# Weight loads pinned to program order in a one-core decoder layer: raw blocks, wide blocks and kept pairs on SyncE's queue

## The chip, the cores and the metric

The kernel runs on one core of a Trainium2 chip. The metric is the device time of one execution in microseconds (us), as the median of several runs. Beside it stands one profiled execution, from which all durations are read.

## The reference

One step of a one-layer hybrid decoder: a prompt of 2048 tokens and 8 samples of 4 tokens, model width 1024, all in float32. Cut to what matters here:

```python
def decoder_layer(x, p, lp, state):
    xn = rms_norm(x, lp['norm_mix_pre'])
    qk_raw, v_m, o_m, gates, q_a, k_a, v_a = split_projection(xn @ lp['w_in'])
    ...                                    # short_conv, heads
    (c_new, n_new, m_new), h = mlstm_prompt(q, k, v, ig, lf)      # or mlstm_chunk on the state
    att = swa_prompt(q_a, k_a, v_a, lp['attn_sinks'])             # or swa_sample on the cache
    y_m = mlstm_output(h, o_m, lp['mlstm_norm'])
    y_a = rms_norm(att.astype(x.dtype), lp['attn_norm'])
    mix = jnp.concatenate([y_m, y_a], axis=-1) @ lp['w_out']
    x = x + rms_norm(mix, lp['norm_mix_post'])
    u = rms_norm(x, lp['norm_ffn_pre'])
    f = jnp.square(jax.nn.relu(u @ lp['w_up'])) @ lp['w_down']
    x = x + rms_norm(f, lp['norm_ffn_post'])
    x = x + jax.nn.sigmoid(x @ lp['w_pgate']) * (p @ lp['w_pproj'])
```

The outputs are the rows of both inputs after the layer, and the new states of both.

## The kernel before, in words

**Stages.** The 16 blocks of 128 prompt rows form six chunks (four of three blocks, two of two). The first part of the kernel runs over the six chunks: norm, the product with w_in, the attention heads and the recurrent heads, whose results go to DRAM (up to about 660 us of the profile). The second part runs over three groups of two chunks. A group goes through the product with w_out (`mix_mm`, matmuls `mo`), the norm behind it (DVE lines 1468 and 1485), the MLP (`mlp`: 16 steps of 256 hidden columns, matmuls `up` and `dn`) and the gate (`gate_mm`, matmuls `pg` and `pv`). The 32 sample rows run beside the prompt: their attention beside group 1, the rest beside the last group.

**Weights.** TensorE reads each weight as a pair of fp32r tiles (high part and rest). `Ring` makes and feeds them. The first time a weight is used, a raw block is loaded from its input (lines 351 to 385; 5 raw buffers), ACT rounds it (line 254) and DVE or POOL subtracts (line 255). If it is used again, POOL stores the pair to DRAM (line 282, `wk<-w`), and every later use is a single load of this kept pair of 512 KB (line 289, `w<-wk`) into one of 7 pair tiles. From the third step of a group's MLP on, the `up` weights of group 0 come from wide blocks of w_up (line 307, four buffers), of which seven sums per step are made on DVE and POOL.

**Queues and order.** All these loads are issued by SyncE (SP in the profile), as are the rows of x (line 477), the decay matrices of the recurrent heads (`Wt<-mbd`, line 961), the gains of the norms behind mix and MLP (`gpost`, `gffn`, line 1453), the rows of p (line 1875) and the last chunk's results (line 1833: `ot` of a prompt block, `ots` of the sample rows). SP takes its instructions in order; one that waits for a buffer or for data holds up all behind it. The kernel's text gives a first order. A scheduler ahead of the run moves instructions of one engine past one another where it expects that to be earlier; `here = tc.keep_in_program_order` takes one instruction out of that and leaves it behind the one that stood just before it on its engine in the text. TensorE's instructions, the subtractions and the stores of pairs are all pinned so; DMAs of SP are not.

**Single buffers beside the ring.** The pool `gp` has one buffer for a gain: the load of `gffn` waits until the last DVE instruction that reads `gpost` (line 1468) has ended. In the text `mlp` asks for `gffn` in its first line, ahead of its first weight:

```python
    gp = es2.enter_context(tc.tile_pool(name="gp", bufs=1, reuse_waits="tile"))
    def mlp(gi, chunks, sample):
        gffn = gain(A["norm_ffn_post"], f"gffn{gi}")
```

In the gate of a chunk, the text has the weights of half 0 (8 of w_pgate, 2 of w_pproj), the results of half 0 (`finish`, whose store waits for ACT and DVE), and then the weights and results of half 1.

Of the kernel before, what the change touches and what calls it, by code (L numbers as in the profile page):

```python
# [11 lines left out]
U32 = mybir.dt.uint32  # L12
# [6 lines left out]
P = 128  # L19
# [11 lines left out]
AD = 64  # L31
# [167 lines left out]
def hybrid_layer(ctx: ExitStack, tc: tile.TileContext, A, O):  # L199
# [4 lines left out]
    dma, put = nc.sync.dma_start, nc.gpsimd.dma_start  # L204
    here = tc.keep_in_program_order
# [47 lines left out]
    def wsplit(hi, lo, src, eng=None):  # L253
        act.copy(hi, src)  # L254
        ins = (eng or weng()).tensor_tensor(lo, src, hi.bitcast(F32), ALU.subtract)  # L255
        if pinned:
            here(ins)

    class Ring:


# [22 lines left out]
        def get(self, key, n, make):  # L284

            t = self.tile(n)
            self.store()
            if key in self.kept:
                dma(t.bitcast(U32), self.kept[key])
            else:  # L290
                make(t[:, 0], t[:, 1])
                if self.uses[key] > 1:
                    self.keep(key, t)
            return t[:, 0], t[:, 1]
# [4 lines left out]
        def product(self, key, i, src):  # L299


            def make(h, l):
                if i == 0:
                    self.blocks = []
                    for e in range(2):
                        t = self.wide.tile([P, KT // 2, 2 * P], F32, tag="w", name=f"{self.nm}b{self.n}{e}")
                        dma(t, src[e * 512 : (e + 1) * 512].rearrange("(k p) n -> p k n", p=P))
                        self.blocks += [t[:, :, :P], t[:, :, P:]]
                a11, a21, a12, a22 = self.blocks
                eng = iter([dve if e == "d" else pool for e in UENG[i]])  # L310
                h, l = [v.rearrange("p (k n) -> p k n", k=4) for v in (h, l)]
                if i == 2:
                    next(eng).tensor_tensor(a21, a21, a22, ALU.add)
                    next(eng).tensor_tensor(a11, a21, a11, ALU.subtract)
                elif i == 3:
                    self.last = self.tile(512)
                    wsplit(*[self.last[:, e].rearrange("p (k n) -> p k n", k=4) for e in range(2)], a22, next(eng))
                    next(eng).tensor_tensor(a22, a22, a11, ALU.subtract)
                elif i == 6:
                    next(eng).tensor_tensor(a12, a12, a11, ALU.subtract)  # L320
                wsplit(h, l, (a11, a12, a11, a22, None, a21, a12)[i], next(eng))

            if i == 4 and key not in self.kept:
                t = self.last
                if self.uses[key] > 1:
                    self.keep(key, t)
                v = t[:, 0], t[:, 1]
            else:
                v = self.get(key, 512, make)
            return [t.rearrange("p (k n) -> p k n", k=4) for t in v]  # L330
# [17 lines left out]
        def row(self, key, src, n):  # L348
            def make(h, l):
                raw = self.load(n)  # L350
                dma(raw, src)
                wsplit(h, l, raw)

            return self.get(key, n, make)

        def heads(self, key, src, j, n):


            def make(h, l):
                raw = self.load(n)  # L360
                for s in range(2):
                    o = s * 256 + j * AD
                    dma(raw[s * AD : (s + 1) * AD], src[o : o + AD])
                wsplit(h, l, raw)

            return self.get(key, n, make)

        def multi(self, key, srcs, kn, n):
            three = lambda v: v.rearrange("p (k n) -> p k n", k=kn)

            def make(h, l):
                raw = self.load(kn * n)
                for off, w, s in srcs:
                    dma(three(raw)[:, :, off : off + w], s)
                wsplit(h, l, raw)

            return [three(v) for v in self.get(key, kn * n, make)]

        def pairs(self, key, segs):


            def make(h, l):
                raw = self.load(512)
                for s, src in enumerate(segs):
                    dma(raw.rearrange("p (k s n) -> p k s n", k=2, s=2)[:, :, s], src)
                v = raw.rearrange("p (k s j c) -> p k j s c", k=2, s=2, j=2)
                h, l = (t.rearrange("p (k j s c) -> p k j s c", k=2, j=2, s=2) for t in (h, l))
                for k in range(2):
                    wsplit(h[:, k], l[:, k], v[:, k])

            return [v.rearrange("p (k n) -> p k n", k=2) for v in self.get(key, 512, make)]
# [1613 lines left out]
```

## Time and profile before

| | |
|---|---|
| median of 3 runs | 2610.94 us (2605.71 to 2612.57) |
| profiled execution | 2623.78 us, span 2621.7 us |
| granted TensorE clock, mean | 0.989 |
| TensorE busy (matmul) | 2534.7 us, 97% |
| DVE, ACT, POOL busy | 57%, 37%, 24% |
| DMA | 651.10 MB, mean 248 GB/s |
| loads of kept pairs | 728 of 512.0 KB and 20 of 528.0 KB, all on SP |

In the rows of the profile the first number is the start of a piece in us from the beginning of the span, then its length, the engine, the line of the kernel, the operation, out<-in and how many are joined; in brackets stands the idle time ahead of it and what ended that. "SPq" is SP's queue of DMA issues: the time of such a row lasts from the first issue to the last one, not to the landing. PEclk is the clock that TensorE was granted, 1.00 being full.

### The profile page before, as it was taken

The page shows a single profiled execution, that of the slowest core. Times are in us where ns is not written, and L with a number is a line of the kernel's source. Part 1 is how long each engine was busy: PE and PEld are TensorE (multiplying, and loading weights), DVE is VectorE, ACT ScalarE, POOL GpSimd, SP SyncE. Part 2 cuts the span into 40 slices and gives each one's busy share as a digit, 9 for nine tenths or more (in the row PEclk, how much of TensorE's full clock was granted, in tenths as well). Part 3 has the DMA queues.
Part 4 walks back from the last instruction along what each step waited for, and adds up shares of the span by engine and source line. Part 5 has one row for each costly group of instructions (what it writes and reads, how often), then busy time and mean ns, then how long its engine had stood idle before and what let it go on. Part 6 is the DMA issues. An engine that isn't in the chain of part 4 may idle for free.

```text
span 2621.7 us, 39337 instructions
## 1 busy us (share of the span) xinstructions
PE 2534.7 (97%) x14260; PEld 2204.3 (84%) x14260; DVE 1483.0 (57%) x3162; ACT 974.3 (37%) x2167; POOL 620.3 (24%) x988
## 2 busy tenths in 40 slices
PE   7999999998999999999999999999999999999998
PEld 7787888777778888888877788999998879999986
DVE  6666656665657655656744654444446346444553
ACT  5545444544445444444523342222223134222231
POOL 5311111112433666666523200000001011000010
PEclk9999999999999999999999999999999999999999
DMA  9756656576898666666799765555556899777787
GB/s 315 273 192 201 207 181 213 194 244 227 260 343 287 254 250 253 244 254 251 271 341 318 255 201 188 188 191 188 187 187 233 295 334 359 253 255 256 256 299 235
DMA packets 220433, 651.10 MB, mean 248 GB/s; under 512 B 25397, under 2 KB 59401, under 8 KB 220224
## 3 DMA queue, kind: packets, MB, share of 16 engines
q1 hardware_dynamic: 170032, 474.02, 53.4%
q0 software_dynamic: 50160, 174.54, 17.3%
q8 instruction: 113, 1.85, 0.3%
q14 instruction: 80, 0.66, 0.1%
q10 hardware_dynamic: 48, 0.03, 0.0%
HBM read 494.34 MB, written 155.25 MB: 248 GB/s over the span
## 4 chain that ended last, share of the span: by engine, by line
PE 77%; DVE 8%; DMA 7%; issue 3%; ACT 2%; POOL 2%; SPq 0%; ACTq 0%; DVEq 0%; POOLq 0%
PE up L148 21%; PE dn L148 21%; PE mo L148 5%; PE pg L148 5%; PE v L148 3%; DMA w<-wk 3%; PE o L148 3%; DMA wk<-w 2%; PE qk L148 2%; PE qa L148 2%; PE gv L148 2%; DVE hl L232 2%; PE aT L152 1%; PE aO L148 1%; PE pv L148 1%
## 5 line engine op out<-in xcount | busy, mean ns | idle before, releaser
L148 PE MATMUL dn<-w,hh 128*128 128x512 f32 x1792 | 564.0, 396 | 6.3 <-ACT re L1654 3.8
L1759 DVE TENSOR_TENSOR f<-f,dn 128x512 f32<-128x512 f32 x420 | 286.9, 686 | 220.5 <-PE dn L148 218.4
L148 PEld LDWEIGHTS dn<-w,hh 128*128 128x128 f32 x1792 | 334.2, 189 | 84.7 <-DVE f L1759 6.8
L148 PE MATMUL dn<-w,hl 128*128 128x512 f32 x896 | 354.5, 396 | 1.6 <-DVE hl L232 1.6
L1734 DVE TENSOR_TENSOR re<-up,re 128x384 f32<-128x384 f32 (+1 forms) x294 | 151.9, 517 | 320.2 <-PE up L148 320.2
L148 PEld LDWEIGHTS dn<-w,hl 128*128 128x128 f32 x896 | 168.8, 188 | 43.5 <-DVE hl L232 5.1
L1735 ACT COPY re<-up 128x384 f32<-128x384 f32 (+1 forms) x42 | 18.8, 448 | 392.0 <-PE up L148 392.0
L1654 ACT ACTIVATE re<-re 128x384 f32<-128x384 f32 (+1 forms) x168 | 83.0, 494 | 207.5 <-DVE re L1734 203.9
L232 DVE TENSOR_TENSOR hl<-re,hh 128x384 fp32r<-128x384 f32 (+1 forms) x192 | 137.6, 717 | 16.8 <-ACT hh L231 15.7
L282 POOL DMA_DIRECT2D wk<-w x242 | 134.1, 556 | 34.4 <-DVE w L255 25.2
L254 ACT CAST w<-wr 128x512 fp32r<-128x512 f32 (+2 forms) x152 | 88.9, 597 | 95.9 <-PE up L148 32.3
L254 ACT CAST w<-wb 128x512 fp32r<-128x512 f32 x98 | 60.6, 620 | 168.4 <-PE dn L148 114.6
L255 POOL TENSOR_TENSOR w<-wr,w 128x512 fp32r<-128x512 f32 (+2 forms) x76 | 100.2, 1319 | 80.5 <-ACT w L254 79.5
L255 POOL TENSOR_TENSOR w<-wb,w 128x512 fp32r<-128x512 f32 x70 | 92.3, 1319 | 110.3 <-ACT w L254 109.8
L1460 POOL DMA_DIRECT2D x<-x1d x16 | 8.7, 545 | 463.5 <-PE up L148 449.4
L1655 ACT ACTIVATE re<-re 128x384 f32<-128x384 f32 (+1 forms) x192 | 94.9, 494 | 5.9
L231 ACT CAST hh<-re 128x384 fp32r<-128x384 f32 (+1 forms) x192 | 92.6, 482 | 8.3
L1067 ACT ACTIVATE s<-s,swt 128x257 f32<-128x257 f32 (+1 forms) x128 | 63.3, 496 | 65.8 <-DVE swt L1064 65.8
L1061 DVE CUSTOM_DVE_ANT_0 s<-aS,cst,sink 128x256 f32<-128x256 f32 (+1 forms) x128 | 57.1, 472 | 52.0 <-PE aS L148 51.6
L148 PE MATMUL up<-t2h,w 128*128 128x384 f32 (+1 forms) x336 | 85.1, 320 | 0.0
L148 PE MATMUL up<-t0h,w 128*128 128x384 f32 (+1 forms) x336 | 85.1, 320 | 0.0
L148 PE MATMUL up<-t1h,w 128*128 128x384 f32 (+1 forms) x336 | 85.1, 320 | 0.0
(1526 smaller groups left out, 6415.7 us busy)
## 6 DMA issues: line engine op xcount, KB each, us to landing
w<-wk SPq DMA_DIRECT2D x728, 512.0 KB, 4.9
wk<-w POOLq DMA_DIRECT2D x238, 512.0 KB, 7.2
wr<-in_w_down_dram SPq DMA_DIRECT2D x64, 256.0 KB, 8.2
wb<-in_w_up_dram SPq DMA_DIRECT2D x28, 512.0 KB, 6.9
w<-wk SPq DMA_DIRECT2D x20, 528.0 KB, 3.9
x<-in_x_prompt_dram SPq DMA_DIRECT2D x16, 512.0 KB, 4.4
y<-yd SPq DMA_DIRECT2D x32, 256.0 KB, 7.0
xr<-in_x_prompt_dram POOLq DMA_DIRECT2D x16, 512.0 KB, 9.4
```

Of the source, the lines that this page charges most:

```text
L148: ins = self.pe.matmul(out, lhsT, rhs, start=start, stop=stop)
L231: act.copy(hi, src)
L232: dve.tensor_tensor(lo, src, hi.bitcast(F32), ALU.subtract)
L254: act.copy(hi, src)
L255: ins = (eng or weng()).tensor_tensor(lo, src, hi.bitcast(F32), ALU.subtract)
L282: here(put(self.kept[key], t.bitcast(U32)))
L1061: dve.tensor_tensor_reduce(s_[:, s, lo : 2 * P], pS[:, s, lo:], bias[:, j, lo:], 1.0 if s == 0 else 0.0625, sink[:, h : h + 1], ALU.add, A ...
L1067: act.activation(e_, e_, AF.Exp, bias=nm[:, s : s + 1], accum_out=sm[:, s : s + 1])
L1654: act.activation(t, src, AF.Relu)
L1655: act.square(t, t)
L1734: add = lambda out, a, b: dve.tensor_tensor(out, a, b, ALU.add)
L1759: dve.tensor_tensor(out(i), out(i), ps, ALU.add)
```

## The change

A new helper `wload` issues a DMA on SP and pins it with `here`. All six places in `Ring` that load weights use it: kept pairs, wide blocks, and the four kinds of raw blocks. Other DMAs of SP stay unpinned, but a pinned load stays behind the instruction that stood just before it on SP in the text, of whatever kind that is.

```diff
--- before.py
+++ after.py
@@ -256,6 +256,10 @@
         if pinned:
             here(ins)
 
+    def wload(out, src):
+
+        here(dma(out, src))
+
     class Ring:
...
@@ -286,7 +290,7 @@
             if key in self.kept:
-                dma(t.bitcast(U32), self.kept[key])
+                wload(t.bitcast(U32), self.kept[key])
...
@@ -304,7 +308,7 @@
-                        dma(t, src[e * 512 : (e + 1) * 512].rearrange("(k p) n -> p k n", p=P))
+                        wload(t, src[e * 512 : (e + 1) * 512].rearrange("(k p) n -> p k n", p=P))
...
@@ -348,7 +352,7 @@
-                dma(raw, src)
+                wload(raw, src)
...
```

The remaining three edits (`heads`, `multi`, `pairs`) are the same one-word change. TensorE's order is the same in both kernels. On SP the order changes in many places; three follow. Of a row the first word is the line, then the operation, out<-in with the number of each tile, and the shape; `w` is a pair tile, `wr` a raw block, `wk` a kept pair in DRAM. The lines of the changed kernel are 4 higher, and its six kinds of weight load all read line 261.

The turn from chunk 0 to chunk 1 of the first part. SP before:

```order
L351 DMA wr_1406<-in_w_in_dram 128x512
L351 DMA wr_1474<-in_w_in_dram 128x512
L351 DMA wr_7677<-in_w_out_dram 128x512
L351 DMA wr_7683<-in_w_out_dram 128x512
L351 DMA wr_7752<-in_w_out_dram 128x512
L351 DMA wr_7759<-in_w_out_dram 128x512
L289 DMA w_1497<-wk_193 128x1056
L289 DMA w_1500<-wk_200 128x1056
L289 DMA w_1503<-wk_208 128x1056
L961 DMA Wt_1414<-mbd_626 128x4x128
```

and SP in the changed kernel:

```order
L261 DMA wr_1406<-in_w_in_dram 128x512
L965 DMA Wt_1414<-mbd_626 128x4x128
L261 DMA wr_1474<-in_w_in_dram 128x512
L261 DMA w_1497<-wk_193 128x1056
L261 DMA w_1500<-wk_200 128x1056
L261 DMA w_1503<-wk_208 128x1056
```

The four raw blocks of w_out have gone to the place where the mix of group 0 uses them, and the decay matrix `Wt_1414` stands ahead of the last raw block of w_in and of the three kept pairs.

The start of group 1's MLP. SP before:

```order
L289 DMA w_15119<-wk_8085 128x1024
L289 DMA w_15153<-wk_8472 128x1024
L289 DMA w_15155<-wk_8478 128x1024
L289 DMA w_15157<-wk_8485 128x1024
L289 DMA w_15159<-wk_8492 128x1024
L289 DMA w_15283<-wk_8621 128x1024
L289 DMA w_15285<-wk_8628 128x1024
L289 DMA w_15287<-wk_8635 128x1024
L1453 DMA gffn_15151<-in_norm_ffn_post_dram 128x1024
```

and SP in the changed kernel:

```order
L261 DMA w_15119<-wk_8085 128x1024
L1457 DMA gffn_15151<-in_norm_ffn_post_dram 128x1024
L261 DMA w_15153<-wk_8472 128x1024
L261 DMA w_15155<-wk_8478 128x1024
L261 DMA w_15157<-wk_8485 128x1024
```

The seven pairs of w_up that stood ahead of the gain now stand behind it (w_15119 is the last pair of w_out). In group 0 likewise: before, `gffn_8465` stood behind all eight raw blocks of w_up (`wr_8468` to `wr_8638`) and three of w_down; now it stands behind the last pair of w_out, `w_8433`, and ahead of `wr_8468`. In group 2 `gffn_20716` stands behind the first six pairs of w_up in both kernels.

The end of the kernel, between half 0 and half 1 of the last gate. SP before:

```order
L289 DMA w_25510<-wk_13675 128x1024
L289 DMA w_25552<-wk_13749 128x1024
L289 DMA w_25554<-wk_13756 128x1024
L289 DMA w_25573<-wk_13781 128x1024
L289 DMA w_25575<-wk_13788 128x1024
L289 DMA w_25595<-wk_13816 128x1024
L289 DMA w_25597<-wk_13823 128x1024
L1833 DMA out_dram<-ot_25531 128x512
L1833 DMA out_dram<-ot_25537 128x512
L289 DMA w_25620<-wk_13848 128x1024
L289 DMA w_25622<-wk_13855 128x1024
L1833 DMA out_dram<-ots_25547 32x512
```

and SP in the changed kernel:

```order
L261 DMA w_25510<-wk_13675 128x1024
L1837 DMA out_dram<-ot_25531 128x512
L1837 DMA out_dram<-ot_25537 128x512
L1837 DMA out_dram<-ots_25547 32x512
L261 DMA w_25552<-wk_13749 128x1024
L261 DMA w_25554<-wk_13756 128x1024
L261 DMA w_25573<-wk_13781 128x1024
```

All three stores of half 0 now stand ahead of all ten pairs of half 1.

More of the change, by code (lines that the diff above doesn't have):

```diff
@@ L362, in make @@
                     o = s * 256 + j * AD
-                    dma(raw[s * AD : (s + 1) * AD], src[o : o + AD])
+                    wload(raw[s * AD : (s + 1) * AD], src[o : o + AD])
                 wsplit(h, l, raw)
@@ L373, in make @@
                 for off, w, s in srcs:
-                    dma(three(raw)[:, :, off : off + w], s)
+                    wload(three(raw)[:, :, off : off + w], s)
                 wsplit(h, l, raw)
@@ L384, in make @@
                 for s, src in enumerate(segs):
-                    dma(raw.rearrange("p (k s n) -> p k s n", k=2, s=2)[:, :, s], src)
+                    wload(raw.rearrange("p (k s n) -> p k s n", k=2, s=2)[:, :, s], src)
                 v = raw.rearrange("p (k s j c) -> p k j s c", k=2, s=2, j=2)
```

## The prediction

> **What bounds the kernel now.** I read the page first: busy times, the chain, the loads.
>
> ```profile
> PE 2534.7 (97%) x14260; PEld 2204.3 (84%) x14260; DVE 1483.0 (57%) x3162; ACT 974.3 (37%) x2167; POOL 620.3 (24%) x988
> PE 77%; DVE 8%; DMA 7%; issue 3%; ACT 2%; POOL 2%; SPq 0%; ACTq 0%; DVEq 0%; POOLq 0%
> w<-wk SPq DMA_DIRECT2D x728, 512.0 KB, 4.9
> ```
>
> TensorE's matmuls fill 97% of the span and make 77% of the chain that ended last, so the kernel gets longer or shorter only by what TensorE (PE) waits for, and by what its clock loses behind a wait. The change leaves PE's order alone and moves only loads. A kept pair lands 4.9 us after its issue (median of 728), so a load that is issued less than that ahead of its matmul costs time. Next come PE's waits, by what ended them:
>
> ```profile
> PE mo L148 <- DMA w<-wk: 5.5, 3, 2.8
> PE qk L148 <- DMA w<-wk: 4.5, 3, 3.9
> PE pg L148 <- DMA w<-wk: 1.8, 1, 1.8
> PE up L148 <- DMA w<-wk: 1.6, 1, 1.6
> ```
>
> Over the whole run the waits put down to kept pairs come to 5.5 + 4.5 + 1.8 + 1.6 = 13.4 us. That is what loads in better turn could return where a wait carries that name. The profiled execution took 2623.78 us (span 2621.7, so 2.1 outside it), 12.8 us or 0.5% above the median of 2610.94. I sum changes on the execution and put them on the median.
>
> **Part 1, the turn from chunk 0 to 1: a gain.** SP's timeline, the chain in order of time, PE's timeline, and a table by stretches:
>
> ```profile
> 114.69 3.58 SPq L289 DMA_DIRECT2D w<-wk  x3
> 118.36 1.20 SPq L961 DMA_DIRECT2D Wt<-mbd  x1
> 115.08 1.12 PE mI L148 x8
> 118.36 8.58 DMA Wt<-mbd
> 139.86 0.32 PE gv L148
> 132.43 1.12 PE L152 MATMUL x31t<-ident,x 128*128 128x128 f32 x4 [2.99 <-ACT os L831]
> 132.50:135.00 2.50, 2.50 (x14) 1.95 (x15) 1.63 (x5) 1.43 (x3) 0.00 (x0) 0.50 0.57 180
> 135.00:137.00 2.00, 2.00 (x12) 1.99 (x12) 1.68 (x4) 0.95 (x2) 0.00 (x0) 0.50 0.72 262
> 137.00:140.00 3.00, 3.00 (x25) 2.42 (x24) 1.60 (x6) 0.81 (x2) 0.70 (x2) 0.76 0.93 329
> ```
>
> The decay matrix Wt is issued at 118.36, behind three kept pairs, and lands 8.58 us later at 126.94. ACT's exponentials of it then hold up ACT's queue until `os`, for which PE waits 2.99 us. The matmuls `mI`, which free the tile, end at 116.20. Moved ahead of the pairs, Wt can be issued there, 2.2 us sooner, with 1.5 MB of pairs no longer ahead of it. It would land near 121 to 123, and the 2.99 us go. The clock (the third column from the end) was 0.50, 0.50 and 0.76 in the 7.5 us behind the wait: 2.5 x 0.5 + 2 x 0.5 + 3 x 0.24 = 3.0 us of work lost. I count 2 of them, since some matmuls there wait for DVE too. Sum -5, ends -3 (the wait alone) and -6. The pairs that now stand behind Wt are chunk 1's, first needed by `gv` at 139.86; issued from 117 on, they have over 10 us to spare.
>
> The Trainium skill, page "TensorE: Matmul & The Clock Gate", part 1, says that the clock is halved after an idle window of about 3.4 us and comes back after about 3.4 us of steady work. The trace halves it after a wait of 2.99 us already. By the page each wait below would cost 1.7 us of clock on top, where I take 2.
>
> **Part 2, mix of group 0: small, both ways.** The first raw blocks of w_out, so far loaded around 100 us, now come at 660 to 680, close to the first `mo`; and w_up's raw blocks no longer mix with the pairs of the second chunk's mix:
>
> ```profile
> 701.00 14.38 SPq L374 DMA_DIRECT2D wr<-in_w_up_dram  x4
> 715.48 9.64 SPq L289 DMA_DIRECT2D w<-wk  x5
> 726.92 1.19 PE L148 MATMUL mo<-w,yt01h 128*128 128x512 f32 x2 [3.73 <-DVE ms L1490]
> 741.54 0.73 PE L148 MATMUL mo<-w,yt01h 128*128 128x512 f32 x2 [1.99 <-DMA w<-wk]
> 720.00:740.00 20.00, 15.82 (x63) 12.02 (x61) 9.72 (x21) 6.48 (x14) 6.51 (x12) 0.83 1.03 411
> 740.00:760.00 20.00, 18.46 (x81) 15.26 (x82) 11.68 (x23) 7.57 (x17) 1.86 (x2) 0.91 0.85 330
> ```
>
> Five raw blocks of w_up held the queue from 701 to 715 and the DMA engines were full (share 1.03, 411 GB/s) while PE waited 3.73 and 1.99 us. The pairs will come first, but most of that traffic is the kernel's own (pairs going to DRAM and back), so I take 2 of the 5.7 us of waits: -2, ends 0 and -10 (all idle time of both stretches, 4.2 + 1.5, and their clock, 15.82 x 0.17 + 18.46 x 0.09 = 4.4). For the late raw blocks of w_out, whose rounding and subtraction stand ahead of `mo`, +1, ends 0 and +4 (about one load).
>
> **Part 3, start of group 0's MLP: a loss.** Now `gffn` stands ahead of all of w_up. SP, PE and DVE, a row of the DMA issues from 756 to 800, and the end of a wait with its stretch:
>
> ```profile
> 773.16 0.33 SPq L1453 DMA_DIRECT2D gffn<-in_norm_ffn_post_dram  x1
> 769.25 0.35 PE L148 MATMUL up<-ut00h,w 128*128 128x384 f32 x1
> 772.46 0.68 DVE L1468 TENSOR_TENSOR f<-f,gpost 128x512 f32<-128x512 f32 x1
> wr<-in_w_up_dram SPq DMA_DIRECT2D x3, 256.0 KB, 3.1
> 795.52 1.22 PE L148 MATMUL dn<-w,hh 128*128 128x512 f32 x2 [3.83 <-ACT re L1654]
> 780.00:800.00 20.00, 16.17 (x80) 14.26 (x79) 17.16 (x27) 12.08 (x25) 10.28 (x13) 0.84 1.00 376
> ```
>
> `gffn` cannot be issued before line 1468 has read `gpost` for the last time, at 773.14, 3.9 us after `up` begins today with weights that are ready. Behind it the first raw block of w_up issues at about 773.5, lands 3.1 us later, is rounded (page: 597 ns on ACT) and has its rest taken (1319 ns on POOL): ready at 778.5. PE waits from 769.25, 9.3 us, and loses 2 of clock. In return the later wait of 3.83 us for w_down, with about 1.6 of clock, goes: its weights have their own queue time while PE stands. 9.3 + 2 - 5.4 = +6, ends +2 (DVE's part done 3 us earlier, since PE leaves its queue alone) and +11 (nothing returned).
>
> **Part 4, wide blocks.** The first wide blocks of w_up move behind kept pairs of w_down, and POOL's first sums change turn. Both ways by at most one load of 4 us; I take -1. The steps behind keep their period, as each load there is issued a whole step ahead.
>
> **Part 5, start of group 1's MLP: a loss.**
>
> ```profile
> 1472.15 16.61 SPq L289 DMA_DIRECT2D w<-wk  x8
> 1490.35 0.33 SPq L1453 DMA_DIRECT2D gffn<-in_norm_ffn_post_dram  x1
> 1489.63 0.69 DVE L1468 TENSOR_TENSOR f<-f,gpost 128x512 f32<-128x512 f32 x1
> 1487.76 0.34 PE L148 MATMUL up<-ut10h,w 128*128 128x384 f32 x1
> w<-wk SPq DMA_DIRECT2D x12, 512.0 KB, 5.2
> 1496.00:1504.00 8.00, 6.51 (x48) 5.59 (x48) 5.96 (x19) 6.70 (x14) 1.66 (x3) 1.00 0.95 349
> ```
>
> Seven pairs of w_up are issued ahead of the gain, so `up` starts at 1487.76 without a gap. `gffn` waits for DVE until 1490.32. With all seven behind it, the first goes out at 1490.7 and lands 5.2 us later (median of the 12 in this window), at 1495.9; if the emptier queue lands it in 3 us, at 1493.7. PE waits 6 to 8.1 us; I take 7.5, plus 2 of clock, less the 1.5 us that PE idles today at 1496 to 1504, which the delay covers: +8, ends +5 and +10. In group 2 the gain keeps its place behind six pairs: 0.
>
> **Part 6, the end: the largest loss.**
>
> ```profile
> 2581.39 15.09 SPq L289 DMA_DIRECT2D w<-wk  x9
> 2596.52 1.58 SPq L1833 DMA_DIRECT2D out_dram<-ot  x2
> 2601.72 0.34 SPq L1833 DMA_DIRECT2D out_dram<-ots  x1
> 2601.01 0.68 DVE L1831 SCALAR_TENSOR_TENSOR ots<-sgs,fs 32x512 f32<-32x512 f32 x1 [1.30 <-DMA out_dram<-ot]
> 2596.42 0.63 PE L148 MATMUL pg<-w,xt21h 128*128 128x512 f32 x2
> 2611.38 1.41 PE pg L148 x6
> ```
>
> Half 1 of the last gate runs on PE from 2596.42 to 2612.79 without a gap, since six of its ten pairs were issued by 2596.48. Now all ten stand behind the store of `ots`, which issues at 2601.72, once DVE has made `ots`, which itself waits for the first store of `ot` to land. The first pair issues at 2602.1 and lands by 3 (an empty queue) to 4.9 us later. Nothing else is left for PE. The wait is 2602.1 + 3.5 - 2596.4 = 9.2, with 2 of clock: +11, ends +8 (stores landing 1.5 us sooner with no pairs beside them, a short landing) and +13.
>
> The page "DMA: Bandwidth & Descriptors", in "Anatomy of one DMA", of the Trainium skill gives 2.0 us plus size over 436 GB/s, fitted for GpSimd's queue: 3.2 us for a pair, an estimate. By it Part 6 would be near +10.7; no transfer of this size runs alone in the trace.
>
> **Parts at nothing.** Later decay matrices, p, x and `gpost` move by a few rows among loads that are issued over 5 us ahead of their use, with PE busy for the time between; if that cover fails, one load of 4.9 us each.
>
> Sum: -5 - 2 + 1 + 6 - 1 + 8 + 11 = **+18 us**: 2641.8 on the execution, 2629 on the median (+0.7%).
>
> **Rivals.** A run says "changed" when it is over 0.3%, 7.8 us, from 2610.94; that is about what a measurement of this kernel can tell.
>
> *Faster.* The raw blocks taken out of the mix's queue free its DMA: Part 2 returns all 10 us, Part 1 5, Part 4 1. For that the three new waits (Parts 3, 5, 6) must cost less than 8 together against my 25: PE would have to find loads landed almost as they are issued. With 6: -10, 2601 us. Against it stand the 4.9 us to landing and the 3.9, 2.6 and 5.3 us by which the three releases come behind PE's need. 0.09.
>
> *Within 0.3%.* Part 2 returns 10, and the three waits cost 16 to 23, near their lower ends: -5 - 10 - 1 + 19 = +3, 2614 us. Or the queue does not hold back where I think it does: the order of the built kernel speaks against that. 0.20.
>
> *A larger loss.* The waits at the MLP's start are not returned later (+5.4 in Part 3, since w_down is late as well; +1.5 in Part 5), and Part 4 goes wrong by 4: 18 + 11 = +29, 2640 us. For it speaks that each late load holds every load behind it on SP. 0.21.
>
> *My sum*, 2629, with its own range 2619 to 2637: 0.50.
>
> So faster 0.09, within 0.3% 0.20, slower 0.71. The range reaches into the second and third rival, 2612 to 2644, and leaves out the faster one and the far end of the losses.
>
> **What would show it.** PE idle 8 to 10 us from about 2596 of the old time to the first `pg` of half 1, with SP's first pair behind `out_dram<-ots`; PE idle 6 to 8 us ahead of the first `up` of group 1, with its first pair behind `gffn`, and 8 to 10 us ahead of the first `up` of group 0; Wt at the first turn landing ahead of 124 and no wait for `os`. Wrong, if PE starts half 1 within 4 us, if `up` in group 1 starts as `mo` ends, or if the waits for kept pairs between 700 and 760 vanish and their clock loss with them.

## The result: slower by 1.8%, and the profile after

The changed kernel takes 2657.61 us (median of 4 runs, 2651.9 to 2659.27); the kernel before took 2610.86 beside it. The ratio is 1.0179 (95% interval 1.0159 to 1.0198), 46.8 us more. The forecast was 2629, with 2612 to 2644 as its range: the direction was right, the size was not.

The page of the changed kernel, its waits of PE by what ended them (us in total, times, the longest; left out are those under 5 us and those that are as long in the kernel before), and its row of kept pairs read:

```profile
PE 2536.9 (96%) x14260; PEld 2206.3 (83%) x14260; DVE 1468.3 (55%) x3162; ACT 973.6 (37%) x2167; POOL 618.6 (23%) x988
PE up L148 <- DVE rq L1523: 12.9, 1, 12.9
PE up L148 <- ACT w L254: 9.4, 1, 9.4
PE pg L148 <- DMA w<-wk: 8.9, 2, 8.0
PE dn L148 <- ACT re L1658: 5.2, 2, 4.5
PE xt20t L152 <- DVE xt00l L232: 5.1, 1, 5.1
w<-wk SPq DMA_DIRECT2D x728, 512.0 KB, 4.8
```

PE's busy time is that of before (2536.9 against 2534.7 us); the time has gone into waits. The first three rows of waits are the places of Parts 5, 3 and 6; `dn` behind `re` (its longest, 4.5 us, stands at the sums of group 1) and `xt20t` (at the gate of group 0) are not in the forecast's sum.

**A second profile of before.** The first profiled execution of the kernel before (2623.78 us) was 12.8 us above its median. So that kernel was profiled once more:

> The kernel before, profiled once more. If its first profiled execution was longer than its median by waits of its own, this one ends 8 to 15 us sooner and the difference has arisen by 1487 us, at the waits ahead of x31t, in the mix of group 0 and at its end. If the profiled times of this kernel are always that long, its span is again 2618 us or more.

It took 2608.22 us, span 2606.1: 15.6 us less, of which 13.4 had arisen by 1473 us. The mix of group 0 is one of the places (5.1 us); the wait ahead of `x31t` is not, since it is no shorter here (3.33 against 2.99 us). PE is busy for 9.4 us less with the same matmuls (2525.3 against 2534.7 us), at a mean granted clock of 0.993 against 0.989. Both kernels issue the same 14260 matmuls in the same order, so the start of the n-th can be compared. The table gives by how much later (+) PE is at the end of each stretch than at its start, against this second profile; places are in its time.

| stretch | changed kernel | first profile of before | forecast |
|---|---|---|---|
| to 139 us (turn of chunk 0 to 1) | -6.6 | +1.1 | -5 |
| to 628 (rest of the first part) | -0.6 | +3.2 | 0 |
| to 760 (mix of group 0) | +2.7 | +5.1 | -1 |
| to 800 (start of group 0's MLP) | +10.9 | +0.8 | +6 |
| to 1252 (steps of that MLP) | -8.0 | -1.0 | -1 |
| to 1306 (gate of group 0) | +8.9 | +0.1 | 0 |
| to 1473 | +0.7 | +4.1 | 0 |
| to 1489 (start of group 1's MLP) | +18.3 | 0 | +8 |
| to 1556 (sums of group 1) | +9.0 | +0.1 | 0 |
| to 2580 | +4.0 | +2.1 | 0 |
| to the end (half 1 of the last gate) | +10.9 | 0 | +11 |
| all | +50.1 | +15.6 | +18 |

What the first profile had in excess lies in the first part and the mixes, where the forecast's Part 2 read its waits. The second profile has 2.48 us there in place of 3.73 and 1.23 in place of 1.99, and a clock of 1.00 (third from the end) where the first had 0.83 and 0.91:

```profile
721.47 0.70 PE L148 MATMUL mo<-w,yt01h 128*128 128x512 f32 x2 [2.48 <-DMA w<-wk]
733.38 0.72 PE L148 MATMUL mo<-w,yt01h 128*128 128x512 f32 x2 [1.23 <-DMA w<-wk]
715.00:735.00 20.00, 16.04 (x74) 12.22 (x73) 12.09 (x29) 8.23 (x17) 6.51 (x12) 1.00 1.03 409
735.00:755.00 20.00, 20.00 (x95) 16.03 (x94) 9.95 (x16) 7.88 (x16) 3.67 (x4) 1.00 0.93 366
```

**Part 1.** Wt is issued at 113.71, 0.05 us behind the last `mI` (first row, of the chain: 112.75 + 0.91), and `x31t` waits 0.54 us, where it waited 3.33 in the second profile of before (last row but two). Behind it the clock, third from the end, is 1.00 (row of 130 to 133 us). The full clock alone does not show the change, though: the last two rows are from the trace of a kernel whose first part is that of before (one pin in group 1, below), and there the clock is 1.00 behind a wait of 3.18 us. Behind the 3.33 us it was 0.50:

```profile
112.75 0.91 PE mI L148 x8
113.71 0.38 SPq L965 DMA_DIRECT2D Wt<-mbd  x1
127.39 0.66 PE L152 MATMUL x31t<-ident,x 128*128 128x128 f32 x4 [0.54 <-ACT os L835]
130.00:133.00 3.00, 3.00 (x31) 2.58 (x28) 2.83 (x12) 1.13 (x3) 0.74 (x2) 1.00 0.90 329
...
131.38 1.11 PE L152 MATMUL x31t<-ident,x 128*128 128x128 f32 x4 [3.33 <-ACT os L831]
131.32 0.66 PE L152 MATMUL x31t<-ident,x 128*128 128x128 f32 x4 [3.18 <-ACT os L840]
131.30:134.70 3.40, 3.38 (x35) 2.91 (x35) 3.40 (x9) 2.49 (x5) 0.00 (x0) 1.00 0.73 240
```

**Part 3, start of group 0's MLP.** SP's timeline, PE's, ACT's, and two stretches with the clock third from the end:

```profile
758.24 0.33 SPq L1457 DMA_DIRECT2D gffn<-in_norm_ffn_post_dram  x1
758.63 10.59 SPq L261 DMA_DIRECT2D wr<-in_w_up_dram  x8
764.25 0.62 ACT L254 CAST w<-wr 128x512 fp32r<-128x512 f32 x1 [0.98 <-DMA wr<-in_w_up_dram]
764.91 0.69 PE L148 MATMUL up<-ut00h,w 128*128 128x384 f32 x1 [9.45 <-ACT w L254]
764.00:770.00 6.00, 4.73 (x14) 4.23 (x15) 1.38 (x5) 3.52 (x6) 3.90 (x6) 0.50 1.05 402
776.00:782.00 6.00, 4.51 (x29) 4.15 (x28) 1.53 (x4) 1.94 (x4) 2.57 (x4) 1.00 1.03 411
```

The wait is 9.45 us (9.3 forecast), by the forecast's chain: gain, raw block, cast. Behind it the raw blocks come one by one from full DMA engines (share 1.05); the clock is 0.50 for 6 us, and PE idles another 1.5 us at 776 to 782. That made 14.5 us in all, of which 3.6 came back.

**Part 4, steps of group 0's MLP.** In the second profile of before (first row) and in the changed kernel (second row), from the pages, DVE's subtraction `hl`, by which the low part of the hidden rows is made:

```profile
L232 DVE TENSOR_TENSOR hl<-re,hh 128x384 fp32r<-128x384 f32 (+1 forms) x192 | 137.4, 716 | 16.0 <-ACT hh L231 15.0
L232 DVE TENSOR_TENSOR hl<-re,hh 128x384 fp32r<-128x384 f32 (+1 forms) x192 | 111.6, 581 | 31.5 <-ACT hh L231 30.4
```

The same 192 subtractions take 25.8 us less (581 instead of 716 ns each). Over these steps (800 to 1252 us) `dn` waits for DVE's `f` and `hl` 4.3 us in all before, and in the changed kernel no longer. The shorter `hl`, 581 to 599 ns, is in each of the eight kernels in which SP's order is new in this MLP, with 5.9 to 8.0 us less over the steps, and in none of the others (713 to 718 ns). So the gain goes with the shorter `hl`; what makes it shorter was not tried.

**The gate of group 0.** SP's, ACT's and PE's timelines in the changed kernel, and (last two rows) DVE's and PE's with pins in group 0's MLP alone, below:

```profile
1282.42 1.94 SPq L1879 DMA_DIRECT2D p<-in_p_prompt_dram  x2
1284.45 11.23 SPq L261 DMA_DIRECT2D wr<-in_w_pgate_dram  x8
1297.16 0.62 ACT L254 CAST w<-wr 128x512 fp32r<-128x512 f32 x1 [4.27 <-DMA wr<-in_w_pgate_dram]
1299.05 1.11 PE L152 MATMUL xt20t<-ident,f 128*128 128x128 f32 x4 [5.12 <-DVE xt00l L232]
...
1281.38 2.35 DVE L255 TENSOR_TENSOR w<-wr,w 128x512 fp32r<-128x512 f32 x2
1284.39 1.11 PE L152 MATMUL xt20t<-ident,f 128*128 128x128 f32 x4 [2.22 <-DVE xt00l L232]
```

In the second profile of before, six raw blocks of w_pgate are issued ahead of the last two loads of `p`; in the changed kernel two are, and eight stand behind these loads, for whose buffer SP waits 10.1 us. ACT then waits 4.27 us for one of the eight, and what DVE needs for `xt20t` stands behind it on ACT. So a late load has its part in the 5.12 us. In the kernel with pins in group 0's MLP alone, ACT waits for no raw block there. DVE makes two subtractions of weights ahead of its part, `xt20t` waits 2.22 us, and the gate still loses 5.8 us (to 1306 us).

**Part 5, start of group 1's MLP.** POOL's, DVE's, SP's and PE's timelines and two stretches:

```profile
1482.08 0.40 PE L148 MATMUL mo<-w,yt11l 128*128 128x512 f32 x1
1484.34 2.15 POOL L1356 DMA_DIRECT2D ssnk<-in_attn_sinks_dram  x4
1486.51 0.57 POOL L1495 TENSOR_TENSOR ms<-ms,nhalf 128x1 f32<-128x1 f32 x1
1487.11 0.75 DVE L1489 SCALAR_TENSOR_TENSOR f<-f,ms,xr 128x512 f32<-128x512 f32 x1 [2.88 <-POOL ms L1495]
1487.78 0.68 DVE L1472 TENSOR_TENSOR f<-f,gpost 128x512 f32<-128x512 f32 x1
1488.49 0.33 SPq L1457 DMA_DIRECT2D gffn<-in_norm_ffn_post_dram  x1
1489.25 22.23 SPq L261 DMA_DIRECT2D w<-wk  x11
1495.36 0.66 PE L148 MATMUL up<-ut10h,w 128*128 128x384 f32 x1 [12.88 <-DVE rq L1523]
1503.95 0.69 PE L148 MATMUL up<-ut10h,w 128*128 128x384 f32 x1 [1.30 <-DMA w<-wk]
1495.50:1508.00 12.50, 10.75 (x31) 9.22 (x32) 0.11 (x1) 1.52 (x3) 0.00 (x0) 0.51 0.82 335
1508.00:1514.00 6.00, 6.00 (x44) 5.68 (x43) 2.84 (x6) 2.76 (x7) 0.00 (x0) 1.00 0.82 252
```

PE waits 12.88 us (the view names a DVE instruction that ended last; the first pair's load behind `gffn` landed then). The last product with `gpost`, which frees the gain's buffer, now stands on DVE behind an instruction that waits for POOL; and POOL issues the loads of the sample rows' attention until 1486.5. So the gain comes 6.0 us behind the last `mo`, and the first pair, issued at 1489.25, is in use 6.1 us later. Then PE waits three times more, the longest 1.30 us, and the clock stays at 0.51 for 12.5 us.

**Part 6, the end.** SP's and PE's timelines and a stretch:

```profile
2624.12 0.33 SPq L1837 DMA_DIRECT2D out_dram<-ots  x1
2624.55 3.26 SPq L261 DMA_DIRECT2D w<-wk  x7
2628.23 1.19 PE L148 MATMUL pg<-w,xt21h 128*128 128x512 f32 x2 [7.97 <-DMA w<-wk]
2628.00:2632.00 4.00, 3.77 (x9) 2.90 (x10) 0.00 (x0) 0.00 (x0) 0.00 (x0) 0.50 1.02 416
```

As forecast: the pairs behind the store, the first in use 3.7 us after its issue, a wait of 7.97 us (9.2 forecast) and a half clock behind it.

### The profile page after: what moved, and what is told of

Read it like the earlier page. It is cut to its first block, busy times and chain, and to the rows that moved or that the text cites. A ratio compares the mean times of both kernels' runs of the same rounds, so it can differ in the third digit from the quotient of the medians.

```text
span 2656.2 us, 39308 instructions
## 1 busy us (share of the span) xinstructions
PE 2536.9 (96%) x14260; PEld 2206.3 (83%) x14260; DVE 1468.3 (55%) x3162; ACT 973.6 (37%) x2167; POOL 618.6 (23%) x988
## 4 chain that ended last, share of the span: by engine, by line
PE 77%; DVE 8%; DMA 7%; issue 3%; ACT 3%; POOL 2%; SPq 0%; ACTq 0%; POOLq 0%; DVEq 0%
PE up L148 23%; PE dn L148 22%; PE pg L148 5%; PE mo L148 4%; DMA w<-wk 3%; PE v L148 3%; PE o L148 2%; PE qk L148 2%; PE gv L148 2%; PE qa L148 2%; DMA wk<-w 2%; PE aT L152 1%; PE aO L148 1%; PE pv L148 1%; PE aS L148 1%
## 5 line engine op out<-in xcount | busy, mean ns | idle before, releaser
L232 DVE TENSOR_TENSOR hl<-re,hh 128x384 fp32r<-128x384 f32 (+1 forms) x192 | 111.6, 581 | 31.5 <-ACT hh L231 30.4
L148 PE MATMUL up<-ut10h,w 128*128 128x384 f32 x288 | 82.7, 354 | 14.6 <-DVE rq L1523 12.9
L148 PE MATMUL up<-ut00h,w 128*128 128x384 f32 x288 | 78.8, 345 | 9.8 <-ACT w L254 9.4
```

The lines of the kernel that those rows point to most:

```text
L148: ins = self.pe.matmul(out, lhsT, rhs, start=start, stop=stop)
L232: dve.tensor_tensor(lo, src, hi.bitcast(F32), ALU.subtract)
```

## Experiments

Two theories were told apart first. A: the loss is made by loads that stand behind DMAs of other kinds. B: it is made by the turn of the loads among one another. Later A was split: A1, only late loads cost; A2, the pins also make the scheduler order unpinned work of ACT and DVE otherwise, and PE waits for that.

**Loads tied to loads alone.**

```diff
-        here(dma(out, src))
+        loads.append(dma(out, src))
+        if len(loads) > 1:
+            tc.add_manual_dep(loads[-1].ins, loads[-2].ins.name, order, reason="load order")
```

> Each weight load is tied to the weight load before it and to nothing else, so the gains and the stores of results are free to stand anywhere. Theory A (the time is lost because loads were tied behind DMAs of other kinds: gffn twice and the last stores): the waits ahead of the first up of groups 0 and 1 and of half 1 of the last gate go, about 10 + 26 + 11 us by the traces, so 2605 to 2615 us. Theory B (the turn of the loads among one another costs, raw blocks being late): only the 11 us of the end go, 2640 to 2650 us.

2602.95 us, ratio 0.9973 (0.9961 to 0.9986): faster than before. The turn among the loads is what the change asked for, and here it is kept; it costs nothing. B falls. In the trace the gain lies in the first 139 us (4.7 us) and in the steps of group 0's MLP (5.9 us, with the shorter `hl`). `Wt` keeps its place behind the pairs, but w_out's raw blocks are gone from ahead of them: it is issued at 114.94, and `x31t` waits 1.20 us.

**The load behind each gffn left unpinned.**

```diff
+        loose.append(gi)          # in mlp, behind gain(...)
-        here(dma(out, src))
+        ins = dma(out, src)
+        if loose:
+            loose.pop()
+        else:
+            here(ins)
```

> As the changed kernel, but the one load that follows each gffn in the text is not pinned (3 of 770 loads). Theory A: both MLP starts are as before, and so is the order of DVE and ACT behind them: 10 + 26 us less than the changed kernel, about 2622 us. Theory B: within 5 us of the changed kernel's 2657.

2631.93 us, ratio 1.0088 (1.0068 to 1.0107): 25.7 us less than the changed kernel. Three loads carry more than half of the loss. A is right on the two waits, but the 36 us expected did not all come: in this kernel's trace PE still falls back 7.7 us at the sums of group 1, whose order on ACT and DVE is still the new one.

**The last results stored by POOL.**

```diff
-        (dma if last else put)(dst, o[:n])
+        put(dst, o[:n])
```

> As the changed kernel, but the last results are stored by POOL, so no pinned load stands behind a store. The order on DVE and ACT is the changed kernel's. Theory A: the wait of PE ahead of half 1 of the last gate goes, 11 us less: about 2647 us. Theory B: no change but the wait's own place, 2655 to 2658 us.

2645.11 us, ratio 1.0137 (1.0121 to 1.0154), 12.5 us less than the changed kernel. Part 6 is shown, by itself and at its size: in the trace the stretch behind 2580 us loses nothing. The start of group 1's MLP, where the orders are the changed kernel's, costs 15.2 us in this trace, not 18.3. The wait is as long (12.98 us), but the clock comes back sooner:

```profile
1496.30:1501.80 5.50, 4.37 (x12) 3.56 (x12) 0.47 (x3) 0.52 (x2) 0.11 (x1) 0.50 1.02 419
1501.80:1508.80 7.00, 5.64 (x31) 5.32 (x32) 0.56 (x1) 1.53 (x3) 0.00 (x0) 1.00 0.95 363
```

**One pin in the kernel before: the first load of w_up in group 1 behind gffn.**

```diff
+            tight.append(gi)      # in mlp, behind gain(...), if gi == 1
+        ins = dma(out, src)
+        if tight:
+            tight.pop()
+            here(ins)
```

> As the kernel before, with a single pin: the first load of w_up in group 1 behind gffn. Theory A with what the traces show (waits, clock and the new order on ACT and DVE behind it): 26 us more than before, 2637 us. Only the wait and its clock, without a new order on ACT and DVE: 19 us more, 2630 us. Theory B: 2611 to 2616 us, since one load is moved and no other turn changes.

2625.24 us, ratio 1.0062 (1.0045 to 1.0079): one load of some 770, and 14.9 us. It is less than either number expected. The sums keep their old order, and DVE keeps the product with `gpost` ahead of the instruction that waits for POOL, so `gffn` is issued 2.4 us behind PE's need, not 6.0. PE waits 10.90 us all the same, and later 1.56, since the first pair is in use only 8.1 us after its issue:

```profile
1475.37 0.33 SPq L1462 DMA_DIRECT2D gffn<-in_norm_ffn_post_dram  x1
1475.80 19.04 SPq L263 DMA_DIRECT2D w<-wk  x9
1483.86 0.66 PE L148 MATMUL up<-ut10h,w 128*128 128x384 f32 x1 [10.90 <-DMA w<-wk]
1491.05 0.44 PE L148 MATMUL up<-ut10h,w 128*128 128x384 f32 x1 [1.56 <-DMA w<-wk]
```

In matmul starts that is 13.3 us against 18.3 in the changed kernel. Of the other 5 us, 2.0 are the longer wait (12.88 against 10.90), which came with the new order on DVE; the rest is clock and short waits, and the trace just above, with the same new order, has 3.1 of it less.

**Pins in group 1's MLP alone, without the one behind gffn.** The edit is that of the second experiment, with `elif now[0] in tight` in place of `else` and a mark `now[0]` set at each stage; `tight` is `["mlp1"]`.

> Loads are pinned in group 1's MLP alone, except the first behind gffn. On SP one load stands three places later, at the MLP's end; on ACT and DVE the sums at 1555 to 1582 us now stand ahead of the work on up's results. Theory A2 (the pins also make the scheduler place unpinned work of ACT and DVE otherwise, and PE waits for that): 7 to 9 us more than before, 2618 to 2620 us, with PE's wait at the first dn behind the sums. Theory A1 (only loads that come late cost): 2610 us, as before.

2616.96 us, ratio 1.0032 (1.0016 to 1.0047), 6.4 us more. In this kernel SP's order differs in one late load only. In its trace (first four rows), and in the second profile of before (last three):

```profile
1541.78 0.83 ACT L1713 CAST t2h<-ts 128x768 fp32r<-128x768 f32 x1 [2.64 <-DVE ts L1708]
1542.64 0.49 ACT L1667 ACTIVATE re<-up 128x384 f32<-128x384 f32 x1
1543.18 0.45 PE L148 MATMUL up<-ut11h,w 128*128 128x384 f32 x1 [0.96 <-ACT re L1667]
1555.06 1.22 PE L148 MATMUL dn<-w,hh 128*128 128x512 f32 x2 [4.25 <-ACT re L1667]
...
1541.25 0.49 ACT L1654 ACTIVATE re<-up 128x384 f32<-128x384 f32 x1 [0.74 <-PE up L148]
1542.76 0.84 ACT L1700 CAST t2h<-ts 128x768 fp32r<-128x768 f32 x1
1545.45 0.49 ACT L1654 ACTIVATE re<-up 128x384 f32<-128x384 f32 x1 [1.85 <-PE up L148]
```

The cast of a sum (`t2h`), which waits 2.64 us for DVE, stands ahead of `re`, the first step on `up`'s result; before it stood behind. `dn` then waits 4.25 us for its hidden rows, and the clock falls to 0.50 (1553 to 1559.6 us). A2 is shown here: a pin on SP, and a loss that no load makes.

**Pins in group 0's MLP alone, without the one behind gffn** (`tight` is `["mlp0"]`).

> Loads are pinned in group 0's MLP alone, except the first behind gffn: the wide blocks stand behind the first raw blocks of w_down of each step, and on DVE the chain of group 0's gate (gffn times f, the transposed halves) stands in another order. Theory A2: about 5 us less in the MLP's steps, then 4 to 9 us more at the gate, where PE waits for DVE ahead of xt20t: 2608 to 2615 us in all. Theory A1: the gate is as before, 2604 to 2606 us. Theory B (the turn of the loads costs): 2615 us or more, lost in the steps of the MLP.

2611.24 us, ratio 1.0008 (0.9996 to 1.002). In its trace PE gains 8.0 us over the steps of the MLP, with the wide blocks behind raw blocks of w_down, and loses 8.2 by the end of the gate behind them (5.8 up to 1306 us, where the table has 8.9 for the changed kernel). The pieces of the changed kernel (-8.0, +8.9) are there, the second somewhat smaller, without the rest of it.

**Pins in the first part alone** (`free` is set where the mix of group 0 begins).

> Loads are pinned in the first part alone (the six chunks). If the gain of 7 to 11 us that the trace of the changed kernel shows up to 660 us is the change's, 2600 to 2603 us. If most of it is what the profiled execution of the kernel before had in excess of its own median, 2605 to 2608 us.

2605.31 us, ratio 0.9983 (0.9972 to 0.9994): 5.3 us, and by the interval 1.6 to 7.3. Part 1 holds with its -5. Of the 11 us that the first pair of traces showed up to 628 us, 4.3 were the first profile's own excess.

**Loads tied to loads, and pinned in the first part.**

> Each weight load is tied to the weight load before it, as in the kernel that came to 2603 us; in the first part it is also pinned behind whatever stood before it, so that Wt goes ahead of the next chunk's pairs. Theory A: the gains of both add, 2 to 3 us less than 2603: 2600 us. If the earlier Wt is worth nothing, 2603 us.

2601.33 us, ratio 0.9969 (0.9959 to 0.9979). It is the fastest of all, and cannot be told from the first experiment's kernel (their intervals overlap).

**All pins, but none behind a DMA that waits.**

```diff
             dma(t, pp_in[b * P : (b + 1) * P, :])
+        if not loose:
+            loose.append(gi)      # and behind gain(...) in mlp; last stores by POOL
```

> As the changed kernel, but the first load behind each gffn and behind each group of loads of p is not pinned, and the last results are stored by POOL: loads are pinned to loads almost everywhere and to no DMA that waits. If the parts add: 2657.6 - 25.7 (gains) - 12.5 (stores) - 3 to -9 (p), so 2610 to 2616 us, with the sums of group 1 still in their new order. If something else in the changed kernel costs time, 2620 us or more.

2624.71 us beside 2612.71 for before, ratio 1.0038 (1.0022 to 1.0054): +12.0, so 35 of the 47 us are gone, above the 2610 to 2616 expected. The term that missed is the one for p: leaving the loads behind p free returned nothing that the times show. PE falls back 6.4 us at the gate of group 0, and fell back 7.0 in the second experiment's trace with p as it was. ACT no longer waits for a late raw block of w_pgate there, but `xt20t` and later `xt40t` wait 2.2 and 2.4 us for DVE.

**The same without pins in group 1's MLP.**

> As the one before, without pins in group 1's MLP, which gives ACT and DVE their old order in the sums there. If that order alone carries the loss there, 6 to 9 us less than the kernel with all pins: 2602 to 2609 us. If not, the same as that kernel.

2614.84 us, ratio 1.0008 (0.9998 to 1.0019), 9.9 us less than the one above: outside the 6 to 9 named, but the step that it tests is confirmed. In the traces the stretch of the sums costs 1.7 us instead of 9.6. The old order of ACT and DVE there is worth 8 to 10 us.

## Why the forecast was wrong, point by point

- **Direction and mechanism: right.** Loads pinned behind a gain that waits for DVE, and behind a store that waits for DVE, leave PE idle; 25.7 and 12.5 us came back when those pins were taken away.
- **Parts at nothing: the step that failed as such.** The forecast took it that the change "moves only loads", and counted what moved on SP. The change also moved work on DVE and ACT that it doesn't touch, and of that the forecast priced only the steps behind raw blocks. Of the 32 us by which the traces exceed the sum (50.1 against 18), 17.9 stand at two places that it put at nothing: the sums of group 1 (9.0) and the gate of group 0 (8.9). The sums are shown by experiment: 6.4 us lost with one load moved on SP, 9.9 us regained with the old order. For the gate the cause stays in part open. A loss of 5 to 9 us is in each of the six kernels with the new order of DVE there and in none of those with the old one, but SP's order is new at that gate in the same six. In the three where the loads behind `p` are pinned, ACT also waits 2.8 to 4.3 us for a late raw block of w_pgate: there the cover that the forecast counted on for `p` did fail. In the other three 5.4 to 6.4 us are lost without that. A kernel with the new order on DVE alone was not tried.
- **Part 5 (+8): mis-sized**, +18.3. Three terms of its sum failed. The release of `gffn` was taken at before's 2.6 us behind PE's need; on the new order of DVE it came 6.0 behind. The first pair was taken to land 5.2 us after its issue or sooner; it was in use after 6.1 us, and after 8.1 where a single pin was set and the release was early. "2 of clock" was read behind a single wait; here 12.5 us ran at 0.51, and PE fell back 7.2 us between the first `up` and the end of that. This last term is not firm: the same order cost 3.1 us less in the trace of the third experiment. Of the return of 1.5 us forecast, 1.9 came.
- **Part 3 (+6): mis-sized**, +10.9. The wait was right (9.45 against 9.3); the clock cost more (0.50 over 6 us, and another wait), and 3.6 instead of 5.4 came back.
- **Part 4 (-1): mis-sized**, -8.0 over the MLP's steps, some 0.5 us a step, seen again in the experiment with group 0's MLP alone. The forecast held that the steps "keep their period"; DVE's `hl` became shorter there, 581 instead of 716 ns.
- **Part 6 (+11): right**, +10.9 in the traces, 12.5 us by experiment, but two of its terms are off and cancel: the wait was 1.2 us shorter than summed (7.97 against 9.2), and the clock cost 2.9 us instead of 2.
- **Part 1 (-5): right**, 5.3 us by experiment and 6.6 in the traces. The wait gave 2.8 us of that. The clock's share is partly luck: behind a wait of 3.0 to 3.3 us it fell to 0.50 in three executions with the old first part (both profiles of before among them) and stayed at 1.00 in two.
- **Part 2 (-1): wrong sign**, +2.7. Its waits of 3.73 and 1.99 us and their clock were read from an execution 15.6 us longer than the second one, where they are 2.48 and 1.23 us, with the clock at 1.00. `mo` waits for kept pairs as long in the changed kernel (3.9 us between 620 and 760 us, 4.0 in the second profile of before), so nothing was returned. Of the 2.7 us, 1.7 are a new wait ahead of the mix's first transposition. The forecast noted the 12.8 us above the median and still used its waits as typical. Its row also has four raw blocks of w_up from 701 to 715 us, not five.
- The 4.0 us between 1556 and 2580 stay open. They are within what the traces differ by there without a cause of this change: the first profile of before has 2.1, and the kernel with pins in group 1's MLP alone 3.8, with only one load moved in that stretch.
- Of the signs, the waits of 9.45 us (8 to 10 named) and 7.97 us (8 to 10 named) came as named, the latter nearly; the one of 12.88 us is longer than the 6 to 8 named. `x31t` still waits 0.54 us for `os`.
- Of the rivals, "a larger loss" came nearest (2640 us), but for other reasons than the ones it named. It added returns that fail, of which 1.8 us in Part 3 did, and a Part 4 that goes wrong, which went the other way. The range's upper end was set by the same omission.

## What to carry to other kernels

A pin "behind what stood before it" ties an instruction to its neighbour of whatever kind: look at what that neighbour waits for, and pin to the last one of the same kind instead. That alone turned 46.8 us of loss into 7.4 of gain. After any change of order, price the differences on all engines that wait, not only on the queue that was edited: a scheduler that sees one load later orders the rest anew. And read stalls from an execution near the median, or from two.

## What the hardware showed that was not expected

In these traces what a wait costs in clock can't be told from its length. Behind the wait of 12.88 us TensorE was granted 0.51 for 12.5 us; with the same order and a wait of 12.98 us it was 1.00 again after 4.4 us, though another 1.17 us of waiting for a pair came later. Behind 10.90 us it was 0.50 for 4.5 us, and behind the 7.97 us at the end, with all seven pairs on their way, 0.50 over the 4 us measured. Behind `x31t` a wait of 3.33 us was followed by 0.50 and one of 3.18 us by 1.00. The Trainium skill, page "TensorE: Matmul & The Clock Gate", part 1, has the clock come back after about 3.4 us of steady work. The traces agree in so far as PE had worked on for 4.0 us behind its last wait (from 1503.95 to 1508 us) when it came back in the first case, and for 4.4 in the second, there with gaps of at most 0.2 us.

Two profiled executions of one program differed by 15.6 us of 2606, most of it in the first part and the mixes of groups 0 and 1. Of the 15.6 us, 9.4 are a longer busy time of PE with the same matmuls. The longer one (2623.78 us) lies above all timed runs of that kernel (2602.86 to 2619.22).
